# Two-layer mixer with differential attention on one core: the keys' copy for the other 64 rows moves from vector operations to a transfer within SBUF

## The chip, the cores and the metric

The kernel runs on one core of one Trainium2 chip. The metric is the device time of one execution in microseconds, as the median of three runs. Engines are named as the profile names them: PE (TensorE), DVE (VectorE), ACT (ScalarE), POOL (GpSimd), and SP (SyncE), which issues the transfers.

## The reference

x is 1 x 512 x 2048 in fp32, with a context of 256 rows. The first block has two layers. In each, a normalised and modulated input goes through a 2048 x 6144 projection into ten parts: four for a short convolution, q, k, v and a gate for attention (eight heads, two halves of 64 rows each for q and k, 128 for v), and two for a multi-scale pool. The three results are joined and projected back. A second block follows. What the change touches is the attention:

```python
def _diff_attn(qb, k_all, v_all, lam):
    s = jnp.einsum('bqhid,bkhid->bhiqk', qb * ATTN_SCALE, k_all)   # i: the two halves
    p = jax.nn.softmax(s, axis=-1)
    a = p[:, :, 0] - lam * p[:, :, 1]
    return jnp.einsum('bhqk,bkhe->bqhe', a, v_all)
```

The result of each head is then divided by its root mean square (line L460 below takes the reciprocal) and multiplied with silu of the gate.

## The kernel before

**Precision.** A product in fp32 is made of three matmuls on float32r operands: each operand is split into a high part, which is the cast, and a low part, which is the value minus the cast (`sub_lo`, L139). `mm3` (L163 to L166) multiplies high by high, high by low and low by high.

**Stages.** Heads run one after the other in `attention` (L465). Per head, four units (`unit`, L198: 16 k steps of matmuls at L166 into a PSUM tile ps_m) make q, k, v and the gate. ps_m has four buffers. Each unit's result is taken out by `evict_q` (L329), `evict_k` (L342), `evict_v` (L359) and silu, and then `attend` (L376) computes for each pair of 128-row query blocks the scores (L394) into one buffer ps_s, their maximum (L399, nb L401) on DVE, the exponential (L408) on ACT, the combination E (L415, L416) on DVE, transposes (L423), the product with v (L433), the squares o2h (ACT) and o2l (DVE, L139), their sum by the matmuls L446 and L447, and the root (L453, L455 on ACT, with a table load) and reciprocal (L460 on DVE).

**The scores' operands.** Row halves hold high and low parts together: Q0 holds in its rows 0 to 63 the high part of the first half of q and in rows 64 to 127 the low part; Q1 the same for the second half with the rows exchanged. To multiply both by the high part of k, and then both by the low part, the key tiles KH0, KL0, KH1 and KL1 need the same 64 rows of k twice, once in each half of the rows. `evict_k` makes all of them from kr (the tile named qr): ACT casts one half of KH0 and KH1 (L350, L351), DVE casts the other (L352, L353), and DVE makes the two halves of KL0 and KL1 with four subtractions (L139, 64 x 768).

**Buffers that tie heads together.** KH and KL have one buffer each, so the eviction of the next head's k waits for the last scores of the head before. The tiles kr, qr and vT share one buffer (tag "qr", bufs=1): the copy of v into vT (L360, L361, on ACT) waits for every reader of kr, the K casts and subtractions. That copy frees the PSUM of the v unit, which a unit of the next head takes.

**Side work.** While attention runs, `advance` feeds in steps of `dots`: POOL multiplies a piece of the next modulation's weights with a vector (gpr, L802), and ACT sums it up (L803); the two exchange one buffer. Weights come by `load_chunk` (L148 to L161): an SP transfer, a cast whi on ACT (L159), and the low part wlo on POOL (L139).

**Order.** The order of the instructions on each engine is set by a scheduler that simulates a timeline of the whole program. So a change of a few lines moves instructions far from it.

Of the kernel before, what the change touches and what calls it, by code (L numbers as in the profile page):

```python
# [12 lines left out]
F32R = mybir.dt.float32r  # L13
# [10 lines left out]
NT = NL + NCX  # L24
# [21 lines left out]
def mixer_stack_kernel(ctx: ExitStack, tc: tile.TileContext, a: dict, out: bass.AP):  # L46
    nc = tc.nc
# [90 lines left out]
    def sub_lo(lo, src, hi, eng):  # L138
        eng.tensor_tensor(lo, src, hi.bitcast(F32), op=ALU.subtract)  # L139
# [182 lines left out]
    def rope(tp, dst, ps):  # L322
        sh = tp.tile([128, NL], F32, name="rsh", tag="rsh", bufs=1)
        nc.vector.stream_shuffle(sh, ps, SWAP16)
        nc.vector.tensor_tensor(dst, ps, rope_c, op=ALU.mult)
        nc.gpsimd.tensor_tensor(sh, sh, rope_s, op=ALU.mult)
        nc.gpsimd.tensor_tensor(dst, dst, sh, op=ALU.add)
# [14 lines left out]
    def evict_k(ap_, aq, u):  # L342
        kr = aq.tile([128, NT], F32, name="qr", tag="qr", bufs=1)
        rope(aq, kr[:, NCX:], u.lat)
        nc.scalar.copy(kr[:, :NCX], u.cx)
        KH0 = ap_.tile([128, NT], F32R, name="KH0", tag="KH0", bufs=1)
        KH1 = ap_.tile([128, NT], F32R, name="KH1", tag="KH1", bufs=1)
        KL0 = ap_.tile([128, NT], F32R, name="KL0", tag="KL0", bufs=1)
        KL1 = ap_.tile([128, NT], F32R, name="KL1", tag="KL1", bufs=1)
        nc.scalar.copy(KH0[0:64], kr[0:64])  # L350
        nc.scalar.copy(KH1[64:128], kr[64:128])  # L351
        nc.vector.tensor_copy(KH0[64:128], kr[0:64])  # L352
        nc.vector.tensor_copy(KH1[0:64], kr[64:128])  # L353
        for half in (slice(0, 64), slice(64, 128)):
            sub_lo(KL0[half], kr[0:64], KH0[0:64], nc.vector)
            sub_lo(KL1[half], kr[64:128], KH1[64:128], nc.vector)
        return (KH0, KL0), (KH1, KL1)

    def evict_v(ap_, u, vT):  # L359
        nc.scalar.copy(vT[:, NCX:], u.lat)  # L360
# [104 lines left out]
    def attention(ap_, aq, l, w, H, Hc, started=None):  # L465
        cx = Hc if l == 0 else None
        T = NT if l == 0 else NL
        for h in range(8):
            if h == 0 and started:
                uq, uk, uv, ug = started  # L470
            else:
                uq = unit(w, 16 + h, H, cx)
            Q = evict_q(ap_, aq, uq, T)
            if not (h == 0 and started):
                uk = unit(w, 24 + h, H, Hc)
            K = evict_k(ap_, aq, uk)
            if not (h == 0 and started):
                uv = unit(w, 32 + h, H, Hc)
            vT = aq.tile([128, NT], F32, name="vT", tag="qr", bufs=1)
            V = evict_v(ap_, uv, vT)  # L480
            if not (h == 0 and started):
                ug = unit(w, 40 + h, H, cx)
            SG = ap_.tile([128, T], F32, name="SG", tag="SG", bufs=1)
            for ps, o, n in ((ug.lat, 0, NL), (ug.cx, NL, NCX)):
                if ps is not None:
                    th = aq.tile([128, NL], F32, name="rsh", tag="rsh", bufs=1)
                    silu2(SG[:, o:o + n], ps, th[:, :n])
            attend(ap_, l, h, Q, K, V, SG, T)
# [804 lines left out]
```

## Time and profile before

| | before |
|---|---|
| runs | 3666.74 us median (3661.18 to 3671.53) |
| profiled execution | 3662.99 us, span 3661.2 us |
| granted TensorE clock, mean | 0.95 of full speed |
| PE, DVE, POOL, ACT busy | 90%, 69%, 56%, 42% |
| attention, layer 0 | about 325 to 1020 us |
| attention, layer 1 | about 1760 to 2345 us |

The profile records one execution on the chip. Busy shares are averages over stages with different limits; what a change in a stage is worth is read from that stage. A row of the timeline gives the start, the duration, the engine, the line and the operation, output before input, and in square brackets how long the engine had sat idle and what ended that. A list of waits gives for each waiting line and each releaser the total in us, the number of waits and the longest.

### The profile page before, as it was taken

The page shows a single profiled execution, that of the slowest core. Times are in us where ns is not written, and L with a number is a line of the kernel's source. Part 1 is how long each engine was busy: PE and PEld are TensorE (multiplying, and loading weights), DVE is VectorE, ACT ScalarE, POOL GpSimd, SP SyncE. Part 2 cuts the span into 40 slices and gives each one's busy share as a digit, 9 for nine tenths or more (in the row PEclk, how much of TensorE's full clock was granted, in tenths as well). Part 3 has the DMA queues.
Part 4 walks back from the last instruction along what each step waited for, and adds up shares of the span by engine and source line. Part 5 has one row for each costly group of instructions (what it writes and reads, how often), then busy time and mean ns, then how long its engine had stood idle before and what let it go on. Part 6 is the DMA issues. An engine that isn't in the chain of part 4 may idle for free.

```text
span 3661.2 us, 47866 instructions
## 1 busy us (share of the span) xinstructions
PE 3285.1 (90%) x16462; PEld 2749.9 (75%) x16462; DVE 2541.2 (69%) x3849; ACT 1543.7 (42%) x3208; POOL 2054.8 (56%) x1420
## 2 busy tenths in 40 slices
PE   5879888889988879999999999999989899999987
PEld 4668677778877767777888888877768787878765
DVE  9994565565547888865555665477566889986676
ACT  4433655666433113233556554422445333335343
POOL 6665666777323453245777773478766544444432
PEclk8889899999999989999999999999999999999999
DMA  7542332233115556664444432287766222222575
GB/s 258 207 164 79 105 98 91 92 98 96 53 64 166 172 167 223 190 221 150 138 146 137 142 124 73 84 304 279 230 221 206 97 89 87 90 81 91 180 226 194
DMA packets 269140, 541.03 MB, mean 148 GB/s; under 512 B 30080, under 2 KB 37088, under 8 KB 260704
## 3 DMA queue, kind: packets, MB, share of 16 engines
q1 hardware_dynamic: 268896, 537.97, 45.0%
q8 instruction: 129, 2.11, 0.2%
q14 instruction: 115, 0.94, 0.1%
HBM read 508.05 MB, written 29.80 MB: 147 GB/s over the span
## 4 chain that ended last, share of the span: by engine, by line
PE 40%; DVE 26%; DMA 12%; issue 9%; POOL 9%; ACT 5%; SPq 1%; POOLq 0%; DVEq 0%; ACTq 0%
PE ps_m L166 30%; DVE acc L985 5%; DMA wraw<-in_w_out_dram 5%; POOL wlo L139 4%; DVE gpr L806 4%; POOL gpr L802 3%; DVE gjunk L292 2%; PE ps_s L394 2%; DVE wlo L139 2%; DMA gw<-in_w_ada_dram 2%; PE ps_v L433 1%; DVE h L139 1%; ACT whi L159 1%; PE ps_m L624 1%; PE ps_m L625 1%
## 5 line engine op out<-in xcount | busy, mean ns | idle before, releaser
L139 POOL TENSOR_TENSOR wlo<-wraw,whi 128x512 fp32r<-128x512 f32 x760 | 1120.2, 1491 | 936.5 <-ACT whi L159 819.8
L166 PE MATMUL ps_m<-h,whi 128*128 128x512 f32 (+1 forms) x4608 | 1571.3, 400 | 67.9 <-ACT vT L360 50.4
L166 PEld LDWEIGHTS ps_m<-h,whi 128*128 128x128 f32 x4608 | 880.4, 193 | 258.4 <-ACT vT L360 52.0
L159 ACT CAST whi<-wraw 128x512 fp32r<-128x512 f32 x1032 | 602.7, 618 | 790.9 <-DMA wraw<-in_w_out_dram 264.8
L166 PE MATMUL ps_m<-h,wlo 128*128 128x512 f32 (+1 forms) x2304 | 919.4, 400 | 0.1
L802 POOL TENSOR_TENSOR gpr<-gw,gv 128x512 f32<-128x512 f32 x320 | 429.6, 1342 | 242.5 <-ACT gpr L803 187.6
L166 PEld LDWEIGHTS ps_m<-h,wlo 128*128 128x128 f32 x2304 | 444.3, 193 | 93.6 <-POOL wlo L139 0.5
L166 PE MATMUL ps_m<-hc,whi 128*128 128x256 f32 x1920 | 510.4, 283 | 0.0
L139 DVE TENSOR_TENSOR wlo<-wraw,whi 128x512 fp32r<-128x512 f32 x272 | 240.4, 896 | 182.0 <-ACT whi L159 179.3
L166 PEld LDWEIGHTS ps_m<-hc,whi 128*128 128x128 f32 x1920 | 356.9, 191 | 4.0
L803 ACT ACTIVATE gpr<-gpr 128x512 f32<-128x512 f32 x320 | 201.6, 630 | 243.9 <-POOL gpr L802 243.1
L166 PE MATMUL ps_m<-hc,wlo 128*128 128x256 f32 x960 | 271.6, 283 | 0.0
L806 DVE SCALAR_TENSOR_TENSOR gpr<-gw,gv 128x512 f32<-128x512 f32 x264 | 263.4, 998 | 10.9 <-DMA gw<-in_w_mod_dram 2.5
L985 DVE SCALAR_TENSOR_TENSOR acc<-gu,pack,acc 128x511 f32<-128x511 f32 (+24 forms) x240 | 232.3, 980 | 5.4
L624 PE MATMUL ps_m<-wlo,y 128*128 128x512 f32 x512 | 207.2, 405 | 21.7 <-POOL wlo L139 13.7
L625 PE MATMUL ps_m<-whi,y 128*128 128x512 f32 x512 | 203.2, 398 | 1.5 <-DVE y L139 1.5
L399 DVE TENSOR_REDUCE mx<-ps_s 128x1 f32<-128x768 f32 (+1 forms) x160 | 135.0, 844 | 84.4 <-PE ps_s L394 83.5
L623 PE MATMUL ps_m<-whi,y 128*128 128x512 f32 x512 | 182.4, 399 | 2.5 <-ACT whi L159 2.3
L166 PEld LDWEIGHTS ps_m<-hc,wlo 128*128 128x128 f32 x960 | 183.4, 191 | 0.8
L240 PE MATMUL ps_m<-h,whi 128*128 128x512 f32 x320 | 126.6, 443 | 56.6 <-DVE h L139 29.1
L428 DVE TENSOR_TENSOR aTl<-ps_t,aTh 128x384 fp32r<-128x384 f32 (+1 forms) x144 | 77.5, 538 | 134.2 <-ACT aTh L427 133.6
L410 DVE RECIPROCAL rd<-dn 128x1 f32<-128x1 f32 x160 | 26.1, 163 | 191.9 <-ACT ps_s L408 99.0
(374 smaller groups left out, 5850.0 us busy)
## 6 DMA issues: line engine op xcount, KB each, us to landing
wraw<-in_w_in_dram SPq DMA_DIRECT2D x640, 256.0 KB, 2.9
wraw<-in_w_out_dram SPq DMA_DIRECT2D x384, 256.0 KB, 3.6
wm<-in_w_mod_dram SPq DMA_DIRECT2D x48, 1024.0 KB, 5.6
gw<-in_w_mod_dram SPq DMA_DIRECT2D x192, 256.0 KB, 3.5
gw<-in_w_ada_dram SPq DMA_DIRECT2D x136, 256.0 KB, 3.2
wm<-in_w_ada_dram SPq DMA_DIRECT2D x14, 1024.0 KB, 6.3
yraw<-yd SPq DMA_DIRECT2D x40, 256.0 KB, 3.4
gw<-in_w_gateT_dram SPq DMA_DIRECT2D x32, 256.0 KB, 3.1
```

The source lines that it names most:

```text
L139: eng.tensor_tensor(lo, src, hi.bitcast(F32), op=ALU.subtract)
L159: nc.scalar.copy(hi[:, sl], raw)
L166: nc.tensor.matmul(ps, w, mv[part], start=(first and p == 0), stop=(last and p == 2))
L240: nc.tensor.matmul(u.lat, wt, H[k][:, part], start=first, stop=last)
L399: nc.vector.reduce_max(mx, sv, axis=AX.XY)
L623: nc.tensor.matmul(ps, yh, hi[:, sl], start=(k == 0), stop=False)
L624: nc.tensor.matmul(ps, yh, lo[:, sl], start=False, stop=False)
L625: nc.tensor.matmul(ps, yl, hi[:, sl], start=False, stop=(k == KT - 1))
L802: nc.gpsimd.tensor_tensor(pr, w, t, op=ALU.mult)
L803: nc.scalar.activation(pr, pr, AF.Copy, scale=scale, accum_out=part[v][:, i:i + 1])
L806: nc.vector.scalar_tensor_tensor(junk, w, scale, t, op0=ALU.mult, op1=ALU.mult, accum_out=part[v][:, i:i + 1])
L985: nc.vector.scalar_tensor_tensor(A[:, s:], U[:, :NL - s], wj(i), A[:, s:], op0=ALU.mult, op1=ALU.add)
```

## The change

In `evict_k` KH and KL of a half become one tile K0 or K1 with two planes (high, low). ACT casts and DVE subtracts only in the 64 rows in which k already lies; the other 64 rows of both planes are then copied from these by a transfer that POOL issues. Per head, two casts and two subtractions on DVE go, and two transfers of 64 x 1536 elements (384 KB) come. In the attention of both layers that is 64 DVE operations and 32 transfers. The casts that ACT makes are the same in number and size. In the changed kernel every line behind this place has a number that is five smaller.

```diff
@@ evict_k
-        KH0 = ap_.tile([128, NT], F32R, name="KH0", tag="KH0", bufs=1)
-        KH1 = ap_.tile([128, NT], F32R, name="KH1", tag="KH1", bufs=1)
-        KL0 = ap_.tile([128, NT], F32R, name="KL0", tag="KL0", bufs=1)
-        KL1 = ap_.tile([128, NT], F32R, name="KL1", tag="KL1", bufs=1)
-        nc.scalar.copy(KH0[0:64], kr[0:64])
-        nc.scalar.copy(KH1[64:128], kr[64:128])
-        nc.vector.tensor_copy(KH0[64:128], kr[0:64])
-        nc.vector.tensor_copy(KH1[0:64], kr[64:128])
-        for half in (slice(0, 64), slice(64, 128)):
-            sub_lo(KL0[half], kr[0:64], KH0[0:64], nc.vector)
-            sub_lo(KL1[half], kr[64:128], KH1[64:128], nc.vector)
-        return (KH0, KL0), (KH1, KL1)
+        Ks = [ap_.tile([128, 2, NT], F32R, name=f"K{m}", tag=f"K{m}", bufs=1) for m in range(2)]
+        for m, Km in enumerate(Ks):
+            own, other = (slice(64 * i, 64 * i + 64) for i in (m, 1 - m))
+            nc.scalar.copy(Km[own, 0], kr[own])
+            sub_lo(Km[own, 1], kr[own], Km[own, 0], nc.vector)
+            nc.gpsimd.dma_start(Km[other], Km[own])
+        return [(Km[:, 0], Km[:, 1]) for Km in Ks]
```

The order of the instructions changes with it. DVE at the third boundary between heads of layer 0, in the kernel before (near 610 to 622 us of its trace):

```order
L352 CAST KH0_4849<-qr_4842 64x768
L399 TENSOR_REDUCE mx_4488<-ps_s_4485 128x1
L428 TENSOR_TENSOR aTl_4453<-ps_t_4480,aTh_4452 128x2x128
L401 TENSOR_SCALAR nb_4490<-mx_4488 128x1
L139 TENSOR_TENSOR KL0_4851<-qr_4842,KH0_4849 64x768 x2
L139 TENSOR_TENSOR o2l_4439<-o2_4436,o2h_4438 128x256
L410 RECIPROCAL rd_4495<-dn_4493 128x1
L415 TENSOR_SCALAR E0_4492<-E0_4492,rd_4495 128x256
L353 CAST KH1_4850<-qr_4842 64x768
L399 TENSOR_REDUCE mx_4500<-ps_s_4497 128x1
L401 TENSOR_SCALAR nb_4502<-mx_4500 128x1
L139 TENSOR_TENSOR KL1_4852<-qr_4842,KH1_4850 64x768 x2
```

and DVE at the same place in the changed kernel:

```order
L394 TENSOR_REDUCE mx_4476<-ps_s_4473 128x1
L396 TENSOR_SCALAR nb_4478<-mx_4476 128x1
L423 TENSOR_TENSOR aTl_4441<-ps_t_4468,aTh_4440 128x2x128
L139 TENSOR_TENSOR K0_4837<-qr_4830,K0_4837 64x768
L139 TENSOR_TENSOR o2l_4427<-o2_4424,o2h_4426 128x256
L405 RECIPROCAL rd_4483<-dn_4481 128x1
L410 TENSOR_SCALAR E0_4480<-E0_4480,rd_4483 128x256
L394 TENSOR_REDUCE mx_4488<-ps_s_4485 128x1
L396 TENSOR_SCALAR nb_4490<-mx_4488 128x1
L139 TENSOR_TENSOR K1_4838<-qr_4830,K1_4838 64x768
```

Both casts and one of each pair of subtractions are gone from between the two maxima; nb and aTl have changed places.

POOL at the same boundary in the changed kernel, with the two transfers (L351) between the side work's products gpr and the weights' low parts wlo:

```order
L797 TENSOR_TENSOR gpr_5922<-gw_5920,gv0_4981 128x512
L351 DMA K0_4837<-K0_4837 64x1536
L797 TENSOR_TENSOR gpr_5925<-gw_5920,gv1_4986 128x512
L139 TENSOR_TENSOR wlo_5648<-wraw_5649,whi_5647 128x512
L139 TENSOR_TENSOR wlo_5648<-wraw_5653,whi_5647 128x512
L351 DMA K1_4838<-K1_4838 64x1536
L797 TENSOR_TENSOR gpr_5930<-gw_5928,gv0_4981 128x512
```

The transfers take places of their own in that queue; in the kernel before it holds only gpr, wlo and the rotations of q and k.

PE where the new head's first unit begins behind that boundary, before and then changed (ps_s_5183 and ps_s_5167 are the new head's first scores):

```order
L394 MATMUL ps_s_4497<-KH1_3894,Q1_3732 128x256
L394 MATMUL ps_s_4497<-KL1_3896,Q1_3732 128x256
L447 MATMUL ps_v_4442<-o2l_4439,ones_r_76 128x256
L166 MATMUL ps_m_5506<-h0_0_131,whi_5508 128x512 x2
...
L423 MATMUL ps_t_4511<-ident_69,E0_4492 128x128 x2
L394 MATMUL ps_s_5183<-KH0_4849,Q0_4694 128x384
```

```order
L389 MATMUL ps_s_4485<-K1_3886,Q1_3724 128x256 x2
L442 MATMUL ps_v_4430<-o2l_4427,ones_r_76 128x256
L418 MATMUL ps_t_4499<-ident_69,E0_4480 128x128 x2
L389 MATMUL ps_s_5167<-K0_4837,Q0_4682 128x384 x4
L166 MATMUL ps_m_5490<-h0_0_131,whi_5492 128x512 x2
```

At this boundary the transposes and the new head's scores have moved ahead of the unit's matmuls. This is so at two of the seven boundaries; at the other five 18 to 24 matmuls of the unit still stand between.

## Rows read from the trace of the kernel before

**Rows 1.** The page: span, then busy us (share of the span) and instructions per engine.

```profile
span 3661.2 us, 47866 instructions
...
PE 3285.1 (90%) x16462; PEld 2749.9 (75%) x16462; DVE 2541.2 (69%) x3849; ACT 1543.7 (42%) x3208; POOL 2054.8 (56%) x1420
```

**Rows 2.** Table by stage: window, length, busy PE, PEld, DVE, ACT, POOL, PEclk, DMA share, GB/s.

```profile
325.00:1002.00 677.00, 604.89 (x3510) 533.16 (x3509) 388.15 (x666) 391.61 (x915) 444.31 (x336) 0.94 0.29 91
1760.00:2345.00 585.00, 567.00 (x3059) 486.74 (x3058) 347.16 (x549) 323.64 (x723) 387.35 (x290) 0.99 0.39 123
```

**Rows 3.** Waits of PE, 325 to 1020 us: total us, times, longest.

```profile
PE ps_m L166 <- ACT vT L360: 50.4, 7, 9.0
...
PE ps_v L447 <- DVE o2l L139: 9.1, 7, 2.3
```

**Rows 4.** Timeline of PE at the third boundary: start, duration, then idle before.

```profile
616.74 0.39 PE L447 MATMUL ps_v<-o2l,ones_r 128*128 128x256 f32 x1 [2.28 <-DVE o2l L139]
623.84 1.22 PE L166 MATMUL ps_m<-h,whi 128*128 128x512 f32 x2 [6.72 <-ACT vT L360]
```

**Rows 5.** Timeline of DVE at the third boundary.

```profile
610.50 1.10 DVE L352 CAST KH<-qr 64x768 fp32r<-64x768 f32 x1 [0.28 <-PE ps_s L394]
...
612.36 2.91 DVE L139 TENSOR_TENSOR KL<-qr,KH 64x768 fp32r<-64x768 f32 x2
...
617.99 1.50 DVE L353 CAST KH<-qr 64x768 fp32r<-64x768 f32 x1
619.41 0.41 DVE L399 TENSOR_REDUCE mx<-ps_s 128x1 f32<-128x256 f32 x1
...
620.04 1.92 DVE L139 TENSOR_TENSOR KL<-qr,KH 64x768 fp32r<-64x768 f32 x2
```

**Rows 6.** Timeline of ACT at the third boundary.

```profile
616.05 0.83 ACT L351 CAST KH<-qr 64x768 fp32r<-64x768 f32 x1
617.16 0.37 ACT L453 COPY rt<-ps_v 128x256 f32<-128x256 f32 x1 [0.28 <-PE ps_v L447]
620.11 0.45 ACT L408 ACTIVATE ps_s<-ps_s,nb 128x256 f32<-128x256 f32 x1 [2.58 <-DVE nb L401]
...
623.22 0.56 ACT L360 COPY vT<-ps_m 128x512 f32<-128x512 f32 x1
```

**Rows 7.** Waits of ACT in layer 0's attention: total us, times, longest.

```profile
ACT gpr L803 <- POOL gpr L802: 128.5, 111, 3.2
```

**Rows 8.** Groups, 325 to 1020 us (busy, mean ns | idle before); then L352's durations (min/median/max).

```profile
L139 DVE TENSOR_TENSOR KL<-qr,KH 64x768 fp32r<-64x768 f32 x32 | 37.6, 1176 | 0.5
L139 POOL TENSOR_TENSOR wlo<-wraw,whi 128x512 fp32r<-128x512 f32 x115 | 158.7, 1399 | 69.0 <-ACT whi L159 68.2 <-PE ps_s L394 0.5
L353 DVE CAST KH<-qr 64x768 fp32r<-64x768 f32 x8 | 8.9, 1109 | 0.3
L352 DVE CAST KH<-qr 64x768 fp32r<-64x768 f32 x8 | 6.5, 814 | 4.3 <-PE ps_s L394 2.4 <-POOL qr L327 1.8
...
L352 DVE CAST KH<-qr x16: 553/800/1637, 333.4 to 2260.1; 64x768 fp32r<-64x768 f32 x16
```

**Rows 9.** Layer 1: the longest of PE's waits, and DVE's row at a boundary.

```profile
PE ps_s L394 <- DVE E L416: 11.2, 5, 3.0
...
1935.48 3.37 DVE L460 RECIPROCAL rt<-rt 128x256 f32<-128x256 f32 x2 [1.06 <-ACT rt L455]
```

**Rows 10.** Table by stage around the third boundary, columns as in rows 2.

```profile
610.00:615.00 5.00, 4.45 (x29) 3.83 (x27) 4.68 (x7) 4.01 (x11) 3.42 (x3) 1.00 0.18 52
...
625.00:630.00 5.00, 5.00 (x15) 3.87 (x14) 2.85 (x5) 1.87 (x6) 2.83 (x3) 0.55 0.15 57
```

**Rows 11.** Transfers: KB each and median us to landing; one issue on SP's timeline.

```profile
yd<-yc SPq DMA_DIRECT2D x4, 384.0 KB, 3.2
...
ca<-in_cc_dram SPq DMA_DIRECT2D x8, 512.0 KB, 7.7
...
619.10 0.33 SPq L798 DMA_DIRECT2D gw<-in_w_mod_dram  x1
```

## The prediction

> **What bounds the kernel now.** Start with the page's head [rows 1]: TensorE (PE) is busy for 90% of the span, VectorE (DVE) for 69%. So a microsecond taken from DVE counts only where PE waits for it. The change touches the attention of the two layers, 325 to 1020 us and 1760 to 2345 us. The table by stage [rows 2] says that in layer 0 PE is idle for 677.0 - 604.9 = 72 us, in layer 1 for only 585 - 567 = 18 us. What those 72 us wait for is in the list of PE's waits [rows 3]: 50.4 us, 7 times, a unit's first matmul (L166) waits for the vT copy on ScalarE (ACT); 9.1 us, 7 times, the L447 matmul waits for o2l on DVE. Seven is the number of boundaries between eight heads. One boundary, the third, shows the mechanism. PE waits 2.28 us for o2l, issues one matmul at 616.74, then waits 6.72 us for vT [rows 4]. vT is written into the buffer that kr has occupied, so it needs every reader of kr done, and it stands in ACT's queue. On ACT [rows 6] the exp at 620.11 had waited 2.58 us for DVE's nb, then a table load, a square root and a gpr step come, and vT at 623.22. On DVE [rows 5] stands, without a gap from 610.50 on, the old eviction of K: two casts and two pairs of subtractions, mixed with the maximum, o2l and E that the exp needs. That queue is what ACT, and through it PE, waits for.
>
> **What goes, layer 0.** At the third boundary DVE loses the cast of 1.10 us, half of the KL pair of 2.91 (1.46), the cast of 1.50 and half of the pair of 1.92 (0.96) [rows 5]: 5.0 us. By the means of all heads it is 0.81 + 1.11 + 2 x 1.18 = 4.3 us per head [rows 8]. The order shows the same four operations gone and the rest of the row in nearly the same sequence (nb and aTl have changed places). What lies ahead of the maximum at 619.41 counts, for the exp waits for it: 1.10 + 1.46 + 1.50 = 4.06 us, the upper end. ACT's own queue sets the lower end: its K cast (616.05 + 0.83) and the rt copy (617.16 + 0.37) end by 617.5, so an exp that waits no more starts no sooner than 617.25 by overlapping as its neighbours do, 620.11 - 617.25 = 2.86 us earlier. The table load, square root and gpr behind it keep their length, so vT comes earlier by the same. I choose 3.5 us, the middle, since the o2l wait in the same stretch (2.28 us, its subtraction stands behind the first KL pair) shrinks as well and lets PE and the rt copy go earlier. Over seven boundaries that is 7 x 3.5 = 24.5 us (20 to 28). What is late next is ACT's row of table load, square root and gpr: about 3.2 of the 6.7 us remain. [...]
>
> **What goes, layer 1.** There the longest item of PE's waits is the score matmul for E on DVE, 11.2 us [rows 9]; no wait for vT of any size is on the list. At a boundary there DVE works on the rt reciprocals [rows 9], no part of the change. Bounds: all of the 11.2 us, or none; a loss could come only by the transfers, priced next. I take 0, because those rows are the nearest.
>
> **What comes, GpSimd.** 32 issues of a 64 x 1536 copy, two per head, stand in GpSimd's (POOL's) queue between gpr and wlo operations. Behind them wait ACT's gpr step (128.5 us of ACT waiting for POOL in 111 waits [rows 7]) and the wlo operations that PE's weights need. No row shows a transfer issued by POOL. The nearest are the 0.33 us of an issue on SP [rows 11] and the 1.40 us of a wlo operation on POOL itself [rows 8]. POOL has cover: in layer 0 its wlo operations waited 68.2 us for whi, over some seven heads 9.7 us per head [rows 8], so two issues of up to 1.4 us each, 2.8 us per head, disappear in it. I count 0; without the cover it is 16 x 0.33 = 5 us to 16 x 1.4 = 22 us for layer 0, and the same again for layer 1.
>
> **What comes, the transfer.** Scores of a new head now need the copied half. 384 KB moved by SP's queue land in 3.2 us (yd), and the slowest listed, 512 KB, in 7.7 us [rows 11]. In the order the new head's first scores stand, at two boundaries, directly behind the transposes; from the issue (behind the K0 subtraction, near 612 us in the old time) to there is about 6 us. At the other five a run of 18 to 24 L166 matmuls stands between, some 14 us at the lower clock. At 3.2 us nothing waits; at 7.7 us two boundaries lose 1.7 us each, 3.4 us. K0 and K1 have one buffer each, as before, so the writes still wait for the previous head's last scores: no new wait there. I take 0, from the yd row, which has the same size.
>
> [...]
>
> **Sum.** The profiled execution took 3662.99 us, its span 3661.2 us. 3663.0 - 24.5 + 0 + 0 + 0 = 3638.5 us. The median of the three runs, 3666.74, lies 3.7 us above the profiled one, so the forecast for a median is 3642 us, with 20 to 28 us of gain 3639 to 3647.
>
> **Rivals.** (A) *The next wait eats the gain.* vT then goes by ACT's queue, where gpr steps waited 128.5 us for POOL [rows 7], and at three boundaries (heads 2, 4 and 5; before at one) the order now has the two rt reciprocals ahead of the K1 subtraction, a reader of kr that vT waits for. A pair of them took 3.4 us in layer 1 [rows 9], as much as the gain of a boundary. With three or more of seven boundaries gaining nothing, and an issue of POOL that costs a little, 0 to 11 us remain: 3656 to 3667 us. For it: the program is reordered widely, PE's row gets shorter pieces. Against it: at the other four no reciprocal is ahead.
>
> (B) *The transfers hold POOL.* [...] POOL then delivers wlo and gpr late, and PE and ACT wait. The cover is 9.7 / 2 = 4.9 us per transfer, and the gain of 3.5 us per head is eaten at (9.7 + 3.5) / 2 = 6.6 us; from there on the kernel is slower. At 10 us each, 2 x 10 - 9.7 = 10.3 us per head, 7 heads: 72 - 24.5 = 48 us more, 3714 us. Against it: 6.6 us is nearly five times a POOL operation of 128 x 512 (1.40 us [rows 8]).
>
> [...]
>
> (C) *The transfer lands late.* It becomes the wait that replaces the cast: scores of the new head wait, and behind them on PE the next unit. Five boundaries have room for 14 us, two for 6 us. At 20 us it is 5 x 6 + 2 x 14 = 58 us, less 24.5: 3700 us. It turns slower when the sum passes 24.5 us, from about 15 us of landing (2 x 9 + 5 x 1 = 23). Against it: no row on the list of transfers is over 7.7 us.
>
> (D) *All of it goes.* vT and o2l stalls both vanish, 50.4 + 9.1 = 59.5 us [rows 3]: 3607 us for a median. Against it: ACT's table load and square root stay ahead of vT.
>
> That the copy replaces nothing is excluded: per head the order has two casts and two subtractions fewer on DVE and two transfers more on POOL.
>
> **How the numbers follow.** Forecast (3639 to 3647) 0.49, A 0.23, B 0.10, C 0.10, D 0.08. A measurement of this kernel can tell about 0.3%, 11 us. Faster: forecast and D, 0.57; within: A, 0.23; slower: B and C, 0.20. The range runs from D's 3607 to C's 3700 and leaves out B's end.
>
> **What would show it.** In the profile after: the casts L352/L353 gone, DVE about 16 x 4.3 = 70 us less busy; PE's wait for the vT copy near 7 x 3.7 = 26 us in place of 50.4; the exp behind the second maximum no longer waiting for nb at the boundaries; layer 1 as long as before. A wait of PE's scores (now L389) for a POOL queue would speak for C; more wlo or gpr waits on POOL, and PE waiting for wlo, for B; ACT's queue ahead of vT unchanged with DVE idle, for A. The prediction is wrong if layer 0's attention isn't shorter by 20 to 28 us, or if layer 1 moves by more than 11 us.

## The result and the profile after

The changed kernel takes 3623.89 us (median of 4 runs, 3616.43 to 3624.87), the one before 3666.48 us: a ratio of 0.988, 95% interval [0.986, 0.9899]. That is 42.6 us faster, on the forecast's side, but by more than the 24.5 us that the sum had: the time lies 15 us below the forecast's own 3639 to 3647 us, and inside the range because that reached down to D's 3607. The profiled execution took 3616.43 us.

The page of the changed kernel; the second line answers to the one of rows 1:

```profile
span 3614.7 us, 47947 instructions
...
PE 3270.7 (90%) x16462; PEld 2740.4 (76%) x16462; DVE 2482.0 (69%) x3785; ACT 1545.9 (43%) x3208; POOL 2064.5 (57%) x1452
```

DVE is 59 us less busy (70 forecast), POOL 10 us more. Where the span's 46.5 us went is read from fixed places in the two timelines. From the first vT copy to the eighth, over seven heads, is "the heads" from here on. The table by stage of the two stretches in which the heads of layer 0, then of layer 1, lie, first of the kernel before:

```profile
338.50:1015.70 677.20, 595.31 (x3460) 524.44 (x3458) 391.05 (x673) 396.03 (x925) 439.85 (x332) 0.93 0.29 90
1765.90:2274.12 508.22, 490.56 (x2688) 423.18 (x2688) 307.34 (x483) 291.52 (x660) 357.16 (x266) 0.99 0.41 127
```

then of the changed kernel:

```profile
337.50:992.40 654.90, 595.18 (x3477) 524.74 (x3476) 362.95 (x645) 395.05 (x923) 442.79 (x348) 0.96 0.35 102
1727.65:2223.21 495.56, 485.47 (x2683) 421.18 (x2682) 287.75 (x455) 291.54 (x658) 358.53 (x281) 0.99 0.50 143
```

In layer 0 PE's busy time is the same and its idle time falls from 81.9 to 59.7 us: 22.3 us gained. In layer 1 the heads are 12.7 us shorter, 7.6 of it idle time of PE and 5.1 busy time. Of the rest, 15 us lie between the heads of layer 0 and those of layer 1 (e2 below says what these are), and 4 us are given back later. The number of matmuls in a stretch, in brackets behind PE's busy time, changes a little with the order, so PE's idle time is the cleaner measure.

PE's waits from 325 to 1020 us in the changed kernel, to be laid beside rows 3:

```profile
PE ps_m L166 <- ACT vT L355: 27.7, 5, 6.5
PE ps_t L418 <- DVE E L411: 7.3, 3, 4.2
...
PE ps_v L442 <- DVE o2l L139: 2.5, 2, 1.7
```

The wait for vT falls by 22.7 us and that for o2l by 6.6; a wait of the transposes for E, 1.3 us before, is 7.3. The fall is not even. At the first and the third boundary, where the order has put the new head's scores ahead of the unit's matmuls, the wait for vT is gone (6.6 and 6.7 us before). At the other five it was 6.7, 6.7, 8.2, 6.5 and 9.0 us and is 6.2, 3.9, 6.5, 5.9 and 5.3. And the third boundary does not come out free: where rows 4 had 2.28 and 6.72 us, PE now waits once, for E:

```profile
613.71 0.55 PE L418 MATMUL ps_t<-ident,E 128*128 128x128 f32 x2 [4.23 <-DVE E L411]
613.92 1.63 PE L389 MATMUL ps_s<-K,Q 128*128 128x384 f32 x4
615.34 1.21 PE L166 MATMUL ps_m<-h,whi 128*128 128x512 f32 x2
```

ACT's timeline at the third boundary, against rows 6, shows the step that the forecast rested on:

```profile
610.35 0.83 ACT L349 CAST K<-qr 64x768 fp32r<-64x768 f32 x1
611.20 0.37 ACT L448 COPY rt<-ps_v 128x256 f32<-128x256 f32 x1
611.60 0.45 ACT L403 ACTIVATE ps_s<-ps_s,nb 128x256 f32<-128x256 f32 x1
...
614.71 0.57 ACT L355 COPY vT<-ps_m 128x512 f32<-128x512 f32 x1
```

The exp no longer has a wait for nb behind it (2.58 us in rows 6): it follows the rt copy directly, so ACT's own row is the floor. From the K cast to vT is 4.4 us; it was 7.2. Over the seven boundaries, the exp ahead of vT waited for nb at six before, 1.65 to 3.83 us, and at one, 1.03 us, after.

The transfers themselves: the line's own view (duration in ns min/median/max, what ended POOL's idle time before it, who waited for it):

```profile
L351 POOL DMA_DIRECT2D K<-K x32: 517/573/753, 336.8 to 2223.5; - x32
...
  DVE rd L405: 9.8, 7
  DVE K L139: 9.3, 4
  DVE nb L396: 5.9, 2
  DVE B_s L316: 2.5, 1
...
  PEld ps_s L389: 0.2, 1
...
DMA to landing us min/median/max: 3.5/4.1/7.3
```

An issue keeps POOL for 0.57 us and a transfer lands in 4.1 us, both in the median; the scores waited for one 0.2 us in all.

### The profile page after: what moved, and what is told of

It is laid out like the page before. It is cut to its first block, busy times and chain, and to the rows that moved or that the text cites. A ratio compares the mean times of both kernels' runs of the same rounds, so it can differ in the third digit from the quotient of the medians.

```text
span 3614.7 us, 47947 instructions
## 1 busy us (share of the span) xinstructions
PE 3270.7 (90%) x16462; PEld 2740.4 (76%) x16462; DVE 2482.0 (69%) x3785; ACT 1545.9 (43%) x3208; POOL 2064.5 (57%) x1452
## 4 chain that ended last, share of the span: by engine, by line
PE 43%; DVE 27%; DMA 12%; issue 8%; POOL 6%; ACT 5%; SPq 0%; DVEq 0%; POOLq 0%; ACTq 0%
PE ps_m L166 32%; DMA wraw<-in_w_out_dram 5%; DVE acc L980 5%; DVE gpr L801 4%; DVE gjunk L292 2%; POOL gpr L797 2%; DVE wlo L139 2%; PE ps_s L389 2%; POOL wlo L139 2%; PE ps_v L428 2%; DVE h L139 2%; ACT whi L159 2%; DMA gv<-in_cc_dram 1%; DVE wm L292 1%; DVE hf L761 1%
## 5 line engine op out<-in xcount | busy, mean ns | idle before, releaser
L166 PE MATMUL ps_m<-h,whi 128*128 128x512 f32 (+1 forms) x4608 | 1569.3, 399 | 36.2 <-ACT vT L355 27.7
L166 PE MATMUL ps_m<-hc,whi 128*128 128x256 f32 x1920 | 518.5, 284 | 0.0
L801 DVE SCALAR_TENSOR_TENSOR gpr<-gw,gv 128x512 f32<-128x512 f32 x264 | 255.6, 968 | 11.4 <-DMA gw<-in_w_mod_dram 3.0
L389 PE MATMUL ps_s<-K,Q 128*128 128x384 f32 x576 | 134.2, 348 | 7.9 <-ACT E L403 6.1
```

The lines of the kernel that those rows point to most:

```text
L166: nc.tensor.matmul(ps, w, mv[part], start=(first and p == 0), stop=(last and p == 2))
L389: nc.tensor.matmul(o, Qm[:, q0:q0 + 128], kp[:, c * ncol:(c + 1) * ncol], start=i == 0, stop=i == 1)
L801: nc.vector.scalar_tensor_tensor(junk, w, scale, t, op0=ALU.mult, op1=ALU.mult, accum_out=part[v][:, i:i + 1])
```

## The experiments

Each is compared with the kernel before on the same chip; the changed kernel is 0.988 on that scale. The runs were spread over several chips, so ratios are to be laid beside each other, not medians. "Heads" are the two stretches above, with PE's idle time in them.

| run | median us | ratio [95%] | heads, layer 0 (PE idle) | heads, layer 1 (PE idle) |
|---|---|---|---|---|
| before | 3666.48 | 1 | 677.2 (81.9) | 508.2 (17.7) |
| changed | 3623.89 | 0.988 [0.986, 0.9899] | 654.9 (59.7) | 495.6 (10.1) |
| e1_dve_kept | 3708.61 | 1.0131 [1.0115, 1.0147] | 692.9 (92.8) | 548.3 (45.2) |
| e2_jitter | 3658.0 | 0.9996 [0.9984, 1.0008] | 679.5 (83.1) | 507.4 (19.5) |
| e3_l0_only | 3634.91 | 0.9931 [0.9912, 0.9951] | 658.4 (61.1) | 509.5 (18.4) |
| e4_l1_only | 3643.22 | 0.9952 [0.9939, 0.9966] | 676.4 (83.1) | 496.1 (10.7) |
| e5_dve_inplace | 3628.65 | 0.9914 [0.9892, 0.9935] | 656.0 (67.6) | 504.2 (19.2) |
| e6_no_copy | 3598.38 | 0.9835 [0.9811, 0.9859] | 637.7 (47.6) | 492.7 (8.6) |
| e7_twice | 3651.79 | 0.9974 [0.9958, 0.9989] | 667.9 (70.6) | 513.3 (24.1) |
| e8_sp_issue | 3622.3 | 0.9893 [0.9873, 0.9912] | 664.1 (65.6) | 491.5 (8.9) |
| e9_vt_before | 3648.57 | 0.9967 [0.995, 0.9983] | | |
| e10_vt_after | 3596.37 | 0.9824 [0.9804, 0.9845] | | |
| e11_mix | 3645.28 | 0.9956 [0.9939, 0.9972] | 669.3 (73.1) | 500.8 (10.8) |
| e12_tiny | 3607.56 | 0.9855 [0.9834, 0.9876] | 649.9 (58.2) | 488.5 (4.3) |

(In e9 and e10 the vT copy stands elsewhere in its head, so the stretches can't be compared.)

### Is it the scheduler's order? e2_jitter

```diff
+        t = ap_.tile([128, 1], F32, name="mx", tag="mx", bufs=4)
+        nc.vector.memset(t, 0.0)
         return (KH0, KL0), (KH1, KL1)
```

> The kernel before with one more DVE operation per head, a memset of one column (about 0.06 us, 16 of them, 1 us in all), which makes the scheduler order the whole program anew with the same work. Theory D: 3661 to 3672 us, as before. Theory O: 10 us or more away from 3666 us, in either direction.

The time is that of before (0.9996), but the run doesn't test what it was made for. Laid side by side, the two traces have the same operations in the same sequence on PE, ACT, POOL and SP; DVE's row differs by the 16 memsets and by one place of a 128 x 1 operation, behind the heads of layer 1. So e2 is a repetition of the kernel before, and it can't tell theory O from D.

What it does show is how far two executions of one order lie apart: 2.3 and 0.8 us in the heads, 6.8 us in the stretch between the heads of layer 0 and those of layer 1 (750.2 and 743.4). In the changed kernel that stretch is 735.2 us, with 24 matmuls fewer in it (3220 for 3244), and PE idles there for 81.4 us, as in e2 (81.2; 88.0 before). No gain of the change is seen in it. A lucky order has to be judged by other runs; the part on why the prediction was right comes back to it.

### Which layer? e3_l0_only and e4_l1_only

```diff
+        if l == 0:      # in e4: l == 1
+            Ks = [ap_.tile([128, 2, NT], F32R, name=f"K{m}", tag=f"K{m}", bufs=1) for m in range(2)]
...
+            return [(Km[:, 0], Km[:, 1]) for Km in Ks]
         KH0 = ap_.tile([128, NT], F32R, name="KH0", tag="KH0", bufs=1)
```

> The new eviction of K in layer 0 alone, the old one in layer 1. The forecast put the whole gain here: 3636 to 3647 us. By the trace after, layer 0's heads gave 23 us and the stretch behind them 8 us: 3633 to 3645 us. Theory O: the gain of layer 1 comes or goes without reference to its eviction, so 3624 or 3655 are as likely.

> The old eviction of K in layer 0, the new one in layer 1 alone. The forecast: nothing, 3661 to 3672 us. If the 15 us that layer 1 is shorter in the trace after come from its DVE work: 3648 to 3656 us. Theory O: anything, and not the complement of the run with layer 0 alone.

Layer 0 alone gives 0.69%, layer 1 alone 0.48%, together 1.17% of the 1.2%: the two parts add up. The forecast's place for the whole gain was right for some 25 us of it and missed some 17. In both runs the heads of a layer follow the row of the kernel whose eviction they have, operation for operation (one matmul at the edge of a stretch aside). So the gain of a layer goes with its own eviction and the order around it; the two are not told apart here. Layer 1's heads are 496 us with the new eviction (495.6 in the changed kernel, 496.1 in e4) and 507 to 510 with the old one (before, e2, e3). Layer 0's heads alike: 655 to 658 against 676 to 680. PE's longest wait in layer 0's attention, first with the new eviction there (e3), then with the old one (e4):

```profile
PE ps_m L166 <- ACT vT L368: 28.3, 7, 6.5
```

```profile
PE ps_m L166 <- ACT vT L368: 50.6, 7, 9.0
```

In layer 1 it is another wait. PE's waits of the changed kernel, 1560 to 2320 us, where rows 9 had 11.2 us of score matmuls waiting for E:

```profile
PE ps_t L418 <- DVE E L411: 6.6, 3, 3.9
```

### Is it DVE's time? e1_dve_kept and e5_dve_inplace

```diff
+        for m, Km in enumerate(Ks):          # e1: a second loop, ahead of the transfers
+            own, other = (slice(64 * i, 64 * i + 64) for i in (m, 1 - m))
+            nc.vector.tensor_copy(Km[other, 0], kr[own])
+            sub_lo(Km[other, 1], kr[own], Km[own, 0], nc.vector)
             nc.gpsimd.dma_start(Km[other], Km[own])
```

> The changed kernel with its transfers, but DVE again makes both casts and both subtractions for the other 64 rows too (the transfer then overwrites them with the same values). Theory D (the freed DVE time at the head boundaries is the gain): back to 3655 to 3670 us, PE's wait for vT in layer 0 45 to 55 us again. Theory O (the scheduler's new order of the whole program is a good part of the gain): well below that, 3625 to 3645 us, or anywhere, with the wait for vT not tied to it.

With DVE's work back, the kernel is 1.3% slower than before: the gain is gone and 49 us more. PE's vT wait in layer 0's heads is 52.6 us, as theory D had it, but the time was outside both expectations. The run isn't clean: each transfer now also has to wait for DVE's cast and subtraction, and it waits at the head of POOL's queue. The transfer's line, and the instruction with which POOL's queue waited before it (ns min/median/max):

```profile
L355 POOL DMA_DIRECT2D K<-K x32: 512/573/731, 336.7 to 2318.2; - x32
L355 POOLq EVENT_SEMAPHORE  x30: 17/2453/7458, 336.2 to 2313.0; - x30
```

In the changed kernel that instruction took 17 ns in the median, at most 417. POOL's idle time in front of its transfers, by the views of the two lines, is 57.3 us here and 27.5 us there. That this is what PE lost is not shown: in the heads no wait of PE's list names a weight or POOL. What has grown in layer 1 (1770 to 2319 us) is PE's wait for SG, which DVE makes, 0.7 us before:

```profile
PE ps_m L166 <- DVE SG L251: 20.2, 6, 4.2
```

So e5 gives DVE work back where no transfer waits for it:

```diff
             nc.gpsimd.dma_start(Km[other], Km[own])
+            for _ in range(2):
+                nc.vector.tensor_copy(kr[own], kr[own])
```

> The changed kernel, with four DVE copies of kr onto itself per head (64 x 768, two behind each subtraction): about the DVE time that the change removed, as readers and writers of kr, but neither K tile nor transfer waits for them. The run with DVE's old work ahead of the transfers came out at 3709 us, slower than before, with POOL's queue waiting up to 7.5 us for each transfer's semaphore. If the excess came from POOL being held by waits for DVE: here only the gain is lost, 3650 to 3670 us, vT's wait near 50 us. If DVE's time alone costs that much: about 3700 us again. If DVE's time is not the cause of the gain: below 3635 us.

The time falls where the expectation had put "DVE's time is not the cause of the gain". DVE is 35.8 us busier than in the changed kernel (2517.8 against 2482.0), well over half of the 59 us that the change had saved; the ratio is 0.9914, some 12 us given back of 43, and its interval overlaps slightly with that of the changed kernel. PE's idle time says more: 360.2 us in the whole span (span less PE's busy time), against 344.0 in the changed kernel and 376.1 before, so half of what the change took off is back. Layer 0's heads only look as short as with the change (656.0): 33 matmuls fewer lie in that stretch, and PE idles 67.6 us in it (59.7). The wait for vT stays low, 26.6 us, but that for E, 7.3 us in the changed kernel, has grown (325 to 1020 us):

```profile
PE ps_t L420 <- DVE E L413: 25.3, 6, 9.3
```

The DVE timeline of the third boundary shows where the copies went:

```profile
614.71 0.53 DVE L353 COPY qr<-qr 64x768 f32<-64x768 f32 x1
...
616.77 0.54 DVE L353 COPY qr<-qr 64x768 f32<-64x768 f32 x1
617.23 0.41 DVE L396 TENSOR_REDUCE mx<-ps_s 128x1 f32<-128x256 f32 x1
...
620.70 0.56 DVE L353 COPY qr<-qr 64x768 f32<-64x768 f32 x1
622.72 0.56 DVE L353 COPY qr<-qr 64x768 f32<-64x768 f32 x1
```

Ahead of the maximum that the exp needs stand 1.07 us of these copies; in the kernel before 4.06 us of the removed work stood there. ACT's exp (618.92 there) again follows its own rt copy without a wait, as at the other boundaries of this run, and the vT copy then waits 1.18 us for a copy of kr. This fits the forecast's step, by which the work counts that stands ahead of that maximum beyond what ACT's own row covers. That nothing else counts isn't shown: the copies cost PE idle time at other places, and the order is new here too.

### What do the transfers cost? e6_no_copy, e7_twice, e8_sp_issue, e12_tiny, e11_mix

```diff
-            nc.gpsimd.dma_start(Km[other], Km[own])        # e6
...
+        Ks = [ap_.tile([128, 2, NT], F32R, name=f"K{m}", tag=f"K{m}", bufs=1) for m in range(2)]     # once per layer
+        for m, Km in enumerate(Ks):
+            nc.vector.memset(Km[64 * (1 - m):64 * (1 - m) + 64].bitcast(F32), 0.0)
```

> The changed kernel without the transfers: the other 64 rows of K0 and K1 hold zeros, set once per layer, so part of the scores is left out; everything else stays. Theory F (the transfers cost nothing, as the forecast counted them): 3617 to 3631 us. Theory P (POOL's issues of 0.57 us, its waits for DVE in front of them, 24 us in all, or late landings cost something): 3600 to 3614 us.

Theory F fell: without the transfers the time is 0.9835, 0.45% (some 16 us) below the changed kernel. Layer 0's heads lose 17.2 us more, layer 1's 2.9. The stretch of layer 0's heads without transfers, beside the one of the changed kernel above:

```profile
336.10:973.80 637.70, 590.08 (x3477) 520.89 (x3476) 354.11 (x643) 392.45 (x923) 436.32 (x332) 0.97 0.30 96
```

PE has 12 us less idle time and 5 us less busy time for the same number of matmuls. The order is new in this run as well, and half of the rows of K hold zeros, so the 16 us are what the kernel without transfers gains, not the price of a transfer by itself.

```diff
+            for _ in range(2):
                 nc.gpsimd.dma_start(Km[other], Km[own])     # e7
```

> The changed kernel with each transfer issued twice, 64 instead of 32. Theory F: 3620 to 3632 us. Theory P: slower by what the first set cost, 3632 to 3645 us; if the second landing delays the scores by 4 us at each head, up to 3690 us.

0.9974, some 34 us above the changed kernel on that scale, between the two estimates of theory P. It does not measure the price of a transfer alone, for the second writes the same rows and waits at the head of POOL's queue for the first to land:

```profile
  DMA K<-K: 45.4, 21
```

That is a row of what ended POOL's idle time in front of the transfers: 45.4 us in which gpr and wlo stood behind it. As in e1, POOL is held by the wait in front of an issue more than by the 0.57 us of the issue. That PE loses its time by this, as the forecast's rival B had it, isn't shown: no wait of PE in the heads names a weight. PE's wait for vT is 36.2 us (325 to 1020 us; 27.7 in the changed kernel), and here the scores waited for a landing, 6.6 us in all.

```diff
-            nc.gpsimd.dma_start(Km[other], Km[own])
+            nc.sync.dma_start(Km[other].bitcast(F32), Km[own].bitcast(F32))     # e8
```

> The changed kernel, the transfers issued by SP (as fp32 bits) and not by POOL. Theory F: the same time, 3617 to 3631 us. Theory P: 5 to 15 us faster. Rival: SP issues in order, and a transfer that waits for DVE holds the weights' transfers behind it as it held POOL; then PE waits for weights, 3640 to 3700 us.

0.9893, not told apart from the changed kernel (0.988). SP's queue waited 46.7 us for DVE in front of the transfers, but neither PE nor ACT waited for a weight's transfer in the heads, so the rival did not come. Theory P's POOL issues are not what is paid, or another cost of the same size has taken their place: PE's wait for vT is 38.3 us (325 to 1020 us; 27.7 in the changed kernel).

```diff
-            nc.gpsimd.dma_start(Km[other], Km[own])
+            nc.gpsimd.dma_start(Km[other, :, :16], Km[own, :, :16])             # e12
...                                                                            # K0, K1 and the zeros as in e6
```

> The changed kernel with transfers of 16 of the 768 columns of each plane, the rest of the other 64 rows zeros set once, so part of the scores is left out: same issues, same waits, next to no data. If the transfers' price (no transfer at all was 1.65% below before, the changed kernel 1.2%) is in data and landing time: 3596 to 3604 us, as without transfers. If it is in the issue and the wait itself, or in the order that the scheduler makes of a transfer: 3610 to 3622 us.

0.9855 lies between e6 and the changed kernel, its interval [0.9834, 0.9876] touches both, and the time is between the two expectations. The heads of layer 0 say more: 649.9 us, of the 17.2 us between the changed kernel and e6 12.2 remain with next to no data, and PE's idle time there is nearly that of the changed kernel (58.2 and 59.7; 47.6 in e6). In layer 0 the price is mostly not in moving the data. Nor is it mostly the wait in front of the issues. POOL's idle time before its transfers in layer 0's heads, first in the changed kernel, then here:

```profile
  DVE K L139: 9.3, 4
  DVE rd L405: 8.7, 6
```

```profile
  issue: 2.9, 3
  DVE K L139: 2.2, 1
```

That wait fell from 18.0 to 5.1 us, and PE's idle time stayed.

```diff
-            nc.gpsimd.dma_start(Km[other], Km[own])        # e11
+            if m == 1:
+                nc.gpsimd.dma_start(Km[other], Km[own])
+            else:
+                nc.vector.tensor_copy(Km[other, 0], kr[own])
+                sub_lo(Km[other, 1], kr[own], Km[own, 0], nc.vector)
```

> The changed kernel with the transfer for K1 alone; K0's other rows are made by DVE as before (one cast and one subtraction more per head). If DVE's time and the transfers' cost add up linearly (62 us gained without transfers, some 18 us paid for them): half of each, 3660 - 31 + 9 = 3638 us. If what is paid is the lateness of K0, which the new head's first scores need: 3605 to 3620 us, a gain on the changed kernel.

0.9956, 7 us above the 3638 us of the linear sum and far from the 3605 to 3620 of a late K0. PE waits 40.2 us for vT (325 to 1020 us), about midway between 27.7 and 50.4. That the lateness of K0's transfer is what is paid finds no support here, nor in the 0.2 us that the scores waited in the changed kernel.

### The link by vT's buffer: e9_vt_before and e10_vt_after

```diff
-            vT = aq.tile([128, NT], F32, name="vT", tag="qr", bufs=1)
+            vT = (
+                aq.tile([128, NL], F32, name="vTl", tag="rsh", bufs=1),
+                ap_.tile([128, NCX], F32, name="vTc", tag="o2", bufs=1),
+            )
...                                          # evict_v copies into the two tiles
```

> The kernel before, with vT in two tiles that share the buffers of rsh and o2 and not that of kr: the vT copy no longer waits for the K casts and subtractions, all of which DVE still makes. Theory L (the link of vT to kr's readers and DVE's queue is what holds PE at the boundaries): vT's wait falls from 50 us to below 25 us, 3625 to 3645 us. Rival (ACT's own queue with its table load, or the exp that waits for DVE, holds vT): the wait stays above 40 us and the time at 3650 to 3662 us.

> The changed kernel with the same other buffers for vT. Theory L: the 27.7 us that PE still waits for vT fall below 15 us, 3595 to 3612 us, below the changed kernel (ratio 0.988, some 3617 us on this chip). Rival: the wait is by now ACT's queue, 3612 to 3624 us.

In e9, the kernel before with the new buffers, PE's wait of a unit's matmul for vT disappears from the list; what leads it then is (325 to 1015 us):

```profile
PE ps_t L424 <- DVE E L417: 31.1, 6, 9.3
PE ps_s L395 <- ACT E L409: 13.2, 6, 3.8
```

and in layer 1, where no unit waited for vT, waits for E and nb grow to 16.6 and 9.6 us. The total is 0.9967, just above what theory L allowed: most of the stall moves to the next product of the same DVE queue. In the changed kernel (e10) DVE has less to do, and there the same edit falls inside theory L's range:

```profile
PE ps_s L390 <- ACT E L404: 11.8, 8, 2.6
PE ps_t L419 <- DVE E L412: 9.8, 3, 5.7
```

No wait for vT is left, and the kernel takes 3596.37 us, 0.9824 [0.9804, 0.9845]: faster than both kernels.

## Why the prediction was right, and where not

**What bounds the kernel, and ACT's row: right.** The wait for vT and through it DVE's queue is where the gain of layer 0 was: vT's wait went from 50.4 to 27.7 us (26 forecast), the exp went to the end of ACT's own row, as the lower end of 2.86 us assumed, and the heads became 22.3 us shorter (24.5 forecast).

**3.5 us at each of seven boundaries: right in the sum, by luck in part.** The third boundary, from which the 3.5 us were worked out, took another course: PE's 2.28 and 6.72 us became one wait of 4.23 us for E; the forecast had 3.2 us left of the wait for vT. By head (from one vT copy to the next) the changes run from 8.1 us shorter to 2.5 us longer, and at three boundaries the wait for vT shrank by only 0.5, 1.7 and 0.7 us. And without transfers (e6) the heads are 39.5 us shorter, so 24.5 against 22.3 is also a gain sized too low beside a cost put at nothing.

**DVE's work or the order?** No run has the changed kernel's order with the old work, so the two are not separated. What speaks against one lucky order: with DVE's work gone and one set of transfers, or none, the changed kernel, e6, e8 and e12 are all faster, 0.9835 to 0.9893. Yet each has an order of its own: in layer 0's heads PE's sequence of operations departs from the changed kernel's at 68, 126 and 116 places, and the changed kernel's from that of before at 152. Where the old work comes back, gain is lost, again in new orders: with half of it 0.9956 (e11), with all of it 1.0131 (e1). e5, with DVE time as large as e11's but elsewhere, loses less, 0.9914.

**Layer 1: wrong.** The step "I take 0, because those rows are the nearest" failed. The prediction had called itself wrong if layer 1 moved by more than 11 us: its heads gave 12.7 us, and its eviction alone 0.48%, some 17 us. The other bound, 11.2 us, was nearer, and still too low. The row for it was there: DVE is 59% busy in that layer (347 of 585 us in rows 2), PE waits for its E five times, and the change takes 20 us of DVE out of the heads. I looked only at whether a K operation stood in the same few microseconds. The 11.2 us wait on E became 6.6 us at other places. PE's idle time in the heads is 17.7 to 19.5 us with the old eviction (before, e2, e3) and 10.1 and 10.7 with the new one (changed, e4), so 7 to 9 us are seen; PE's busy time fell by 5 us, of which a repetition of the old order (e2) shows 3 too. By which operations the freed time reaches E, and where the rest of the 17 us lies, isn't shown.

**POOL and the transfers at nothing: wrong.** The durations were foreseen (0.57 us to issue, within 0.33 to 1.4; 4.1 us to landing, within 3.2 to 7.7), PE waited 0.2 us for a transfer, and still leaving the transfers out gains another 0.45%, some 16 us. A wait that no row of PE shows had been counted at zero. Taking away one thing at a time did not bring them back: not K0's transfer (e11), not POOL's issue (e8), and in layer 0 not the data and most of the wait in front of the issues (e12). What is left is the other order that the scheduler makes around a transfer, and no run isolates it. This stays open.

**So the sum was right in sign and short in size by two errors of opposite sign.** Without transfers the kernel gains 1.65% of 3660, 60 us, not 24.5; with them about 16 less. With the 11.2 us bound of layer 1 the sum would have stood at 3663 - 24.5 - 11.2 = 3627 for the profiled execution.

**The rivals.** A did not come in the total, though some of it did: PE's waits for E, aTh and nb grew to 4 to 7 us each, and three boundaries kept most of their wait for vT. B did not decide here; e1 and e7 show POOL held by a transfer that waits, but not that PE waits for POOL's products. C is out: 7.3 us was the slowest landing (the 14 us that it gave the unit's matmuls ahead of the scores, an estimate with the clock of 0.55 of rows 10 throughout, were 5.8 to 7.4 in the changed kernel). D's end, 3607 us, is as far from the result as the forecast is, but its mechanism did not come: vT's wait did not vanish. In e10 it does, by the other buffer.

## What to carry to other kernels

An operation on a busy engine is worth at least what stands ahead of the next value that another engine waits for, less what that engine's own row covers (here an estimate of 2.86 us at the third boundary; over seven the heads of layer 0 became 22.3 us shorter); look for that value at every place where the engine feeds the bound, not only where the removed operation stands. A transfer that takes an engine's place can cost more than its issue and landing show: the kernel without transfers was 0.45% faster, while the scores had waited 0.2 us for one. A control for a new order has to be looked at before it is used: e2 was meant to be one and kept the old order. And where a copy waits for the readers of a buffer it shares, giving it another buffer can move the stall to the engine behind it: the buffer alone gave 0.3%, on top of the change 0.6% (the change alone 1.2%, both 1.8%; the difference between 0.3 and 0.6 is within the intervals).

## What the runs showed of the hardware

**Most DVE casts took longer beside POOL.** In the kernel before, of the 32 DVE casts of 64 x 768 the 8 that no POOL operation overlapped took 0.55 to 0.56 us, the 24 that one did 1.14 us in the mean, up to 1.64, though four of them took 0.55 to 0.56 as well (worked out from the timelines of both engines). The extreme is in e5, where two copies of 0.56 us took 8.40 us beside a row of POOL operations with no pause:

```profile
1868.17 8.40 DVE L353 COPY qr<-qr 64x768 f32<-64x768 f32 x2
```

```profile
1867.29 2.01 POOL L139 TENSOR_TENSOR wlo<-wraw,whi 128x512 fp32r<-128x512 f32 x1
1869.23 0.58 POOL L351 DMA_DIRECT2D K<-K  x1
1869.84 1.31 POOL L139 TENSOR_TENSOR wlo<-wraw,whi 128x512 fp32r<-128x512 f32 x1
1871.10 1.30 POOL L799 TENSOR_TENSOR gpr<-gw,gv 128x512 f32<-128x512 f32 x1
1872.37 2.54 POOL L139 TENSOR_TENSOR wlo<-wraw,whi 128x512 fp32r<-128x512 f32 x2
1874.88 1.27 POOL L799 TENSOR_TENSOR gpr<-gw,gv 128x512 f32<-128x512 f32 x1
```

So DVE's removed casts had a price that went with POOL's work beside them: 1.14 us in the mean with it, 0.55 to 0.56 us without. What holds a cast up is not shown, nor why four of the 24 were not slowed. POOL's transfers: an issue took 517 to 753 ns in the changed kernel, and landing 3.5 to 7.3 us, against 3.5 to 6.3 us for the same transfers from SP (e8).

**A transfer within SBUF.** In the changed kernel 384 KB from 64 rows to 64 other rows landed in 4.1 us in the median, 3.5 at best, counted from the issue.
